# Batch norm with ReLU: small first pieces of x, and stores issued from ScalarE's queue

## The chip, the cores and the metric

One core of one Trainium2 chip. The metric is device microseconds of a whole execution, the median over repeated runs. All timed runs here are in the fast state with a granted clock of 1.0, and the kernel before runs beside every experiment on the same chip. A profile gives the *span*, from the first to the last instruction, which is 1.7 to 2.1 us shorter than the time, depending on the kernel. Ratios are the mean time of one kernel's fast runs over that of the other's of the same rounds, so not quite the ratio of the medians that are quoted.

## The reference

```python
x: (32, 128, 32, 32) float32; gamma, beta, running_mean, running_var: (128,)
normalized = (x - running_mean[None, :, None, None]) / np.sqrt(running_var[None, :, None, None] + eps)
scaled = normalized * gamma[None, :, None, None] + beta[None, :, None, None]
return np.maximum(scaled, 0)
```

16.8 MB come in and 16.8 MB go out; per element there is one multiply-add and a maximum.

## The kernel before

Each of the 128 partitions takes 16 consecutive rows of 1024 numbers, twice. All of x fits into SBUF, so all loads are issued first. The parameters are spread over the partitions by a small matmul, turned into one scale and one bias per row, and each row is one ReLU ACTIVATE on ScalarE. Loads and stores share SyncE's queue.

```python
J = 16
PIECES = ((0, 8), (8, 16))
...
for t in range(T):                                   # T = 2
    for a, b in PIECES:
        xt = data.tile([P, b - a, HW], F32, name=f"x{t}_{a}")
        nc.sync.dma_start(out=xt, in_=xr[t, :, a:b, :])
        tiles.append((t, a, b, xt))
...                                                  # raw: 4 loads of 0.5 KB on nc.scalar
nc.tensor.matmul(cols..., rep..., raw...)            # then Sqrt, reciprocal, scale_t, bias_t
for t, a, b, xt in tiles:
    for j in range(a, b):
        nc.scalar.activation(out=xt[:, j - a, :], in_=xt[:, j - a, :], func=ACTF.Relu,
                             bias=bias_t[:, j : j + 1], scale=scale_t[:, j : j + 1])
    nc.sync.dma_start(out=outr[t, :, a:b, :], in_=xt)
```

## Time and profile before

| | before |
|---|---|
| time, median of 3 | 84.79 us (84.72 to 84.86) |
| span | 83.2 us |
| 16 DMA engines busy with x and out | 95.5% |
| ScalarE busy | 46% |
| first ReLU, last ReLU ends | 14.9, 52.6 us |
| last load landed, last store landed | 43.4, 82.1 us |

The prediction shows the profile lines behind this and reads them. A data packet here is one partition's share of one DMA: 8 rows of 4 KB make a packet of 32 KB.

### The profile page before, as it was taken

What the parts mean: (1) busy time and instruction counts of PE and PEld (TensorE: products, weight loads), DVE (VectorE), ACT (ScalarE), POOL (GpSimd) and SP (SyncE); (2) the same over time, 40 slices, a digit from 0 to 9 for tenths busy, and PEclk for the clock granted to TensorE, in tenths of its full rate; (3) what the DMA queues carried; (4) which work ended last, traced back from release to release, by engine and by line L of the source; (5) the groups of instructions that cost most, each with busy time, mean ns of one, the idle gap of its engine ahead of it and who ended that gap; (6) DMA issues with size and microseconds to landing.
All of it is one profiled execution on the core that took longest, in us unless ns stands there. A gap on an engine that the chain in (4) does not pass through costs nothing.

```text
span 83.2 us, 115 instructions
## 1 busy us (share of the span) xinstructions
PE 0.7 (1%) x2; PEld 0.5 (1%) x2; DVE 0.8 (1%) x5; ACT 38.0 (46%) x34; POOL 0.8 (1%) x6
## 2 busy tenths in 40 slices
PE   0000003000000000000000000000000000000000
PEld 0000002000000000000000000000000000000000
DVE  0000002100000000000000000000000000000000
ACT  0600001899999999999949999200000000000000
POOL 3000000000000000000000000000000000000000
DMA  5879996997999799899969997998999799899960
GB/s 158 347 331 426 505 457 299 504 504 331 426 504 457 315 489 504 347 410 504 252 284 473 489 457 331 489 489 363 426 489 457 315 489 489 378 410 489 489 268 0
DMA packets 1216, 33.56 MB, mean 404 GB/s; under 512 B 192, under 2 KB 192, under 8 KB 192
## 3 DMA queue, kind: packets, MB, share of 16 engines
q1 hardware_dynamic: 1152, 33.55, 95.5%
q10 hardware_dynamic: 64, 0.00, 0.0%
HBM read 16.78 MB, written 16.78 MB: 404 GB/s over the span
## 4 chain that ended last, share of the span: by engine, by line
DMA 50%; ACT 10%; SPq 1%; ACTq 1%; issue 0%
DMA x<-in_x_dram 50%; ACT x L92 10%; SPq L50 1%; ACTq L130 1%
## 5 line engine op out<-in xcount | busy, mean ns | idle before, releaser
L92 ACT ACTIVATE x<-x,bias_t,scale_t 128x1024 f32<-128x1024 f32 x32 | 36.4, 1226 | 2.2 <-DMA x<-in_x_dram 1.2
L80 ACT ACTIVATE std_t<-cols,eps_t 128x16 f32<-128x16 f32 x1 | 0.3, 273 | 9.8 <-PE cols L72 9.8
L80 ACT ACT_TABLE_LOAD x1 | 1.3, 1283 | 2.6 <-issue 2.6
L72 PE MATMUL cols<-raw,rep 8*128 8x64 f32 x2 | 0.7, 428 | 12.9 <-DMA raw<-in_beta_dram 12.9
L72 PEld LDWEIGHTS cols<-raw,rep 8*128 8x128 f32 x2 | 0.5, 304 | 12.9 <-issue 12.9
L62 POOL TENSOR_SCALAR_AFFINE_SELECT rep<-rep 8x128 f32<-8x128 f32 x1 | 0.4, 393 | 0.1
L82 DVE RECIPROCAL rstd_t<-std_t 128x16 f32<-128x16 f32 x1 | 0.3, 253 | 13.0 <-ACT std_t L80 13.0
L61 POOL MEMSET rep<- 8x128 f32 x1 | 0.2, 194 | 0.3 <-POOLq L116 0.3
L84 DVE TENSOR_TENSOR scale_t<-cols,rstd_t 128x16 f32<-128x16 f32 x1 | 0.2, 174 | 0.1
L86 DVE TENSOR_TENSOR ms_t<-cols,scale_t 128x16 f32<-128x16 f32 x1 | 0.2, 174 | 0.0
L88 DVE TENSOR_TENSOR bias_t<-cols,ms_t 128x16 f32<-128x16 f32 x1 | 0.2, 174 | 0.0
L116 POOL MEMSET const-bfloat16-1.0<- 128x1 bf16 x1 | 0.1, 106 | 0.0
L116 POOL MEMSET const-uint8-127<- 128x1 uint8 x1 | 0.1, 106 | 0.0
L116 POOL MEMSET const-float32-0.0<- 128x1 f32 x1 | 0.1, 103 | 0.3 <-issue 0.3
L116 POOL MEMSET const-float32-1.0<- 128x1 f32 x1 | 0.1, 103 | 0.0
L59 DVE MEMSET eps_t<- 128x1 f32 x1 | 0.1, 59 | 0.9 <-PEq L116 0.9
## 6 DMA issues: line engine op xcount, KB each, us to landing
x<-in_x_dram SPq DMA_DIRECT2D x4, 4096.0 KB, 26.0
out_dram<-x SPq DMA_DIRECT2D x4, 4096.0 KB, 29.6
raw<-in_running_var_dram ACTq DMA_DIRECT2D x1, 0.5 KB
raw<-in_gamma_dram ACTq DMA_DIRECT2D x1, 0.5 KB
raw<-in_running_mean_dram ACTq DMA_DIRECT2D x1, 0.5 KB
raw<-in_beta_dram ACTq DMA_DIRECT2D x1, 0.5 KB
```

Of the source, the lines that this page charges most:

```text
L50: nc.sync.dma_start(out=xt, in_=xr[t, :, a:b, :])
L61: nc.gpsimd.memset(rep, 1.0)
L62: nc.gpsimd.affine_select(out=rep, in_=rep, compare_op=mybir.AluOpType.is_equal, fill=0.0, base=0, pattern=[[0, P // Q], [-1, Q]], channel ...
L72: nc.tensor.matmul(cols.rearrange("p k j -> p (k j)"), rep.rearrange("q r s -> q (r s)"), raw.rearrange("q k j -> q (k j)"), start=True, s ...
L80: nc.scalar.activation(out=std_t, in_=cols[:, 0, :], func=ACTF.Sqrt, bias=eps_t[:, 0:1], scale=1.0)
L82: nc.vector.reciprocal(out=rstd_t, in_=std_t)
L84: nc.vector.tensor_mul(out=scale_t, in0=cols[:, 1, :], in1=rstd_t)
L86: nc.vector.tensor_mul(out=ms_t, in0=cols[:, 2, :], in1=scale_t)
L88: nc.vector.tensor_sub(out=bias_t, in0=cols[:, 3, :], in1=ms_t)
L92: nc.scalar.activation(out=xt[:, j - a, :], in_=xt[:, j - a, :], func=ACTF.Relu, bias=bias_t[:, j : j + 1], scale=scale_t[:, j : j + 1],)
L116: nc = _bacc.Bacc("TRN2", target_bir_lowering=False, num_devices=1)
L130: with _tile.TileContext(nc) as tc:
```

## The change

Its intent: let the first rows arrive early, compute them early and write them while the rest of x is still being loaded.

```diff
-PIECES = ((0, 8), (8, 16))
+PIECES = (((0, 2), (2, 4), (4, 8), (8, 16)), ((0, 8), (8, 16)))
@@
-        for a, b in PIECES:
+        for a, b in PIECES[t]:
@@
-        nc.sync.dma_start(out=outr[t, :, a:b, :], in_=xt)
+        nc.scalar.dma_start(out=outr[t, :, a:b, :], in_=xt)
```

## The prediction

> **What bounds the kernel now.** I read the page from the top: busy shares first, then the queues, then the waits, then stretches of the span.
>
> ```profile
> PE 0.7 (1%) x2; PEld 0.5 (1%) x2; DVE 0.8 (1%) x5; ACT 38.0 (46%) x34; POOL 0.8 (1%) x6
> ...
> q1 hardware_dynamic: 1152, 33.55, 95.5%
> q10 hardware_dynamic: 64, 0.00, 0.0%
> ```
>
> No compute engine is near full; ScalarE, which does all the arithmetic, is busy 46% of 83.2 us. The queue of x and of the results (q1, fed by SyncE) holds the 16 DMA engines for 95.5% of the span. 33.55 MB in 1152 packets is 1024 data packets of 32 KB (8 DMAs of 128 partitions) and 128 closing ones, so 64 data packets per engine.
>
> The waits of SyncE's queue tell the order in which that traffic runs:
>
> ```profile
> SPq L99 <- ACT x L92: 37.4, 4, 11.0
> SPq L130 <- DMA out_dram<-x: 29.2, 1, 29.2
> SPq L99 <- DMA x<-in_x_dram: 11.1, 2, 10.3
> ```
>
> The middle row is the end of the kernel: after the last store is issued, SyncE waits 29.2 us for it to land. ScalarE has long finished; the timeline has its last stretch:
>
> ```profile
> 14.90 27.25 ACT L92 ACTIVATE x<-x,bias_t,scale_t 128x1024 f32<-128x1024 f32 x24 [1.02 <-DVE bias_t L88]
> 24.09 28.81 SPq L99 DMA_DIRECT2D out_dram<-x  x4
> 43.39 9.16 ACT L92 ACTIVATE x<-x,bias_t,scale_t 128x1024 f32<-128x1024 f32 x8 [1.23 <-DMA x<-in_x_dram]
> ```
>
> The first store is issued at 24.09 but stands behind the loads in the same queue, so nothing is written until the last load has landed at 43.4. Compute ends at 43.39 + 9.16 = 52.6, about 30 us before the end. The chain of waits (50% on the loads of x, 10% on ScalarE) stops at that compute and gives no reason for the 30 us after it; the stretches do:
>
> ```profile
> 0.00:1.80 1.80, 0.00 (x0) 0.00 (x0) 0.06 (x1) 0.00 (x0) 0.80 (x6) 1.00 0.00 0
> 1.80:3.60 1.80, 0.00 (x0) 0.00 (x0) 0.00 (x0) 1.05 (x1) 0.00 (x0) 1.00 1.00 291
> 3.60:13.30 9.70, 0.38 (x2) 0.41 (x2) 0.00 (x0) 0.24 (x1) 0.00 (x0) 1.00 1.00 433
> 13.30:23.00 9.70, 0.27 (x2) 0.08 (x1) 0.78 (x4) 8.37 (x9) 0.00 (x0) 1.00 1.00 432
> ...
> 37.50:43.70 6.20, 0.00 (x0) 0.00 (x0) 0.00 (x0) 4.97 (x6) 0.00 (x0) 1.00 1.03 370
> 43.70:53.40 9.70, 0.00 (x0) 0.00 (x0) 0.00 (x0) 8.84 (x8) 0.00 (x0) 1.00 1.00 432
> ```
>
> The last two columns are the DMA share and GB/s. Loads alone run at 432 GB/s, stores alone too, with the engines full. The holes are 1.8 us before the first byte, a slow first packet (1.8 us at 291, so 0.6 us lost), and the handover from loads to stores (6.2 us at 370: 6.2 x (1 - 370/432) = 0.9 us lost). Thus 33.55 MB / 432 GB/s = 77.7 us, plus 1.8, 0.6 and 0.9, is 81.0; the rest, some 2.2 us, is the spread between engines, the last landing and the closing barrier. The kernel is bound by DMA bytes at an already flat rate.
>
> **What the Trainium skill says.** Four places.
> "DMA: Bandwidth & Descriptors", section "Issuing engines are not separate DMA queues": DMAs started from scalar, sync or gpsimd run on the same 16 engines and interleave; a second issuer saves only issue time. The trace agrees as far as it goes: while q10 is served, the stretch 3.60 to 13.30 is at a total of 433 GB/s.
> The same page, "Queues, rings and completion order": each DMA engine goes round-robin over the queues with work, a packet at a time. The trace fits: the parameters are 64 packets on q10, and though the last is issued at 2.08 and is half a KB, the matmul waits for it until 12.9, about one 1.2 us turn per packet.
> The same page, section "Bandwidth", puts the fabric ceiling at 435 GB/s; the 432 above stands at it.
> "Perfetto Trace Analysis", "Per-instruction lifecycle": an ACTIVATE waits for its semaphore in a wait queue while the sequencer reads on, whereas a DMA instruction waits in the sequencer itself. No row of this trace shows what that does to a store queued behind an ACTIVATE.
>
> **The change, part by part.**
> (1) Smaller first loads. The first two are 8 KB per partition, then 16 KB, then 32 KB thrice: 6 loads and 6 stores for 4 and 4. Four more DMAs add closing packets only, far under 0.2 us. A 32 KB packet takes 32768 x 16 / 432e9 = 1.21 us, so an 8 KB one 0.3 us: the parameters, interleaved with those, should arrive between 5 and 9 us instead of 12.9. From matmul start to first ReLU was 14.90 - 12.92 = 2.0 us, so ScalarE starts the ReLUs at 7 to 11 instead of 14.9. That is 4 to 8 us gained on an engine that finishes 30 us early: worth nothing directly.
> (2) Stores on ScalarE's queue. SyncE's loads no longer stand in front. ReLUs start 27.25 / 24 = 1.13 us apart, so the first store (two rows) goes out at 10 to 14 and its bytes run beside the loads. The instruction order shows most stores one ACTIVATE after their piece, with that ACTIVATE waiting for the next load; so a store may go out only when the next piece has landed. An issue takes 0.3 to 0.6 us of ScalarE's sequencer, 6 of them about 2.5 us, off the bounding path.
> (3) Loads get later. Each byte of store taken early pushes a load back. With alternating packets, an 8 KB store packet gets a fifth of the bytes beside 32 KB loads. Stepping the packets by hand in this order, the last load lands near 50 us instead of 43.4. By then (50 - 2) x 432 = 20.7 MB have moved, 16.8 of loads, 3.9 of stores; 12.9 MB of stores, 30 us of work, are left, against 9.2 us of ReLUs and some 3 us of landing and issue for the last piece. DMA does not run dry.
> (4) Two late loads now wait for parameter semaphores that they reuse. Those arrive by 9 us, and the loads issued before them last until about 22 us: no hole.
> Sum: bytes unchanged, 77.7 us; start and end unchanged; the handover of 0.9 us is either paid again when mixing begins, or saved: 0 to -0.9; packets and issues +0.1. Median 84.0 to 84.9.
>
> **The rivals.**
> A: mixing costs rate. The handover shows loads slowed while stores begin to be fetched. If it is paid again for each 32 KB of store that runs beside loads, about 8 packets per engine before 50 us (3.9 MB / 16 / 32 KB), it is 8 x 0.9 = 7 us: about 92. A fraction of it is as plausible, 86 to 88. For: those 0.9 us appear only where the directions meet. Against: a one-time filling of the engine's buffer would look the same. The before trace has no steady mix, so this is the real uncertainty.
> B: bytes rather than packets are shared evenly. Then half the rate goes to stores from 12 us, the last load lands at about 68, nearly all other stores are written by then, and the last piece's 9.2 us of ReLUs stand bare ahead of its 9.7 us store: span about 91. The parameters' one-by-one delay speaks against it.
> C: stores fall behind in ScalarE's queue because of the ACTIVATE ahead. The backlog of 30 us hides it; it would cost only if B held too.
> D: overlap gains. All it could win is handover 0.9 and a slow first packet 0.6, together 1.5 us, or 1.8%: under the 2% line.
>
> **Range and chances.** The centre is 84.7: no net change, a little of the handover saved, a little mixing loss. Low 83.2 is D in full; high 88.5 leaves room for half of A. Faster by over 2% needs under 83.1, beyond D: 0.05. A or B in full or by a third gives slower: 0.28. The rest, 0.67, is the same.
>
> **What the changed profile would show.** Right: parameters landing well before 12.9, ReLUs from 7 to 11 us, ScalarE busy still 38 us but spread to near 60 with waits for loads, reads and writes mixed from about 12 us at 425 to 432 GB/s, last load near 50, DMA share at 95%, the end again a wait for a store to land. A shows as a lower rate with the DMA share still full, in the mixed stretch alone. B shows as a late last load (past 60) and a hole in DMA ahead of the last store. The prediction is wrong if the mixed stretch holds under 415 GB/s, or if any hole over 1.5 us opens.

## The result, and the profile after

The changed kernel takes 84.17 us (84.12 to 84.31, 4 runs) against 84.83 (84.72 to 84.89, 4 runs) before: ratio 0.9927, 95% interval 0.991 to 0.9944. It is a small gain of 0.7%, clear of noise and inside the 2% band. The span fell from 83.2 to 82.3 us.

Everything that the change was meant to do, it did. First the two queues of the changed kernel, which now share the traffic:

```profile
q1 hardware_dynamic: 864, 16.78, 48.6%
q10 hardware_dynamic: 928, 16.78, 47.5%
```

48.6% and 47.5% together are 96.1%: the engines were full before and are full now. Then its waits by engine (us in total, times, longest); the first row is ScalarE waiting for loads, the second the matmul waiting for the parameters:

```profile
ACT x L92 <- DMA x<-in_x_dram: 14.4, 3, 6.3
...
PE cols L72 <- DMA raw<-in_beta_dram: 7.4, 1, 7.4
```

The parameters came at 7.4 us instead of 12.9. ScalarE now waits 14.4 us for loads, where it waited 1.2: it computes the first pieces early and is then held up by loads that share the engines with stores. The timeline shows the same (start, length, instruction, in square brackets the idle time before it):

```profile
9.38 3.50 ACT L92 ACTIVATE x<-x,bias_t,scale_t 128x1024 f32<-128x1024 f32 x3 [1.03 <-DVE bias_t L88]
11.78 0.38 ACTq L99 DMA_DIRECT2D out_dram<-x  x1
...
24.87 9.16 ACT L92 ACTIVATE x<-x,bias_t,scale_t 128x1024 f32<-128x1024 f32 x8 [6.33 <-DMA x<-in_x_dram]
37.00 1.24 ACT L92 ACTIVATE x<-x,bias_t,scale_t 128x1024 f32<-128x1024 f32 x1 [2.97 <-DMA x<-in_x_dram]
37.00 0.34 ACTq L99 DMA_DIRECT2D out_dram<-x  x1
...
51.21 1.24 ACT L92 ACTIVATE x<-x,bias_t,scale_t 128x1024 f32<-128x1024 f32 x1 [5.05 <-DMA x<-in_x_dram]
51.21 0.34 ACTq L99 DMA_DIRECT2D out_dram<-x  x1
...
60.39 0.34 ACTq L99 DMA_DIRECT2D out_dram<-x  x1
```

ReLUs start at 9.38 and the first store goes out at 11.78, against 14.90 and 24.09. But the last load lands at 51.2 instead of 43.4, and the last store is issued at 60.39, where it was 52.6 before. Early work at one end has become late work at the other, as it must when the engines have no spare time. Note also the pairs at 37.00 and 51.21, to which experiment 3 returns: the fourth piece was computed by 24.87 + 9.16 = 34.03, yet its store went out at 37.00, with the ACTIVATE ahead of it.

The stretches tell whether mixing costs rate (last column GB/s):

```profile
13.30:52.10 38.80, 0.00 (x0) 0.00 (x0) 0.00 (x0) 24.45 (x22) 0.00 (x0) 1.00 1.02 432
52.10:71.50 19.40, 0.00 (x0) 0.00 (x0) 0.00 (x0) 8.26 (x8) 0.00 (x0) 1.00 1.00 432
```

432 GB/s with loads and stores mixed, 432 with stores alone.

**Where 0.9 us of span went.** One part is at the very end. SyncE closes the kernel by checking the DMA semaphores, mostly two at a time. Here is that row of the kernel before, then of the changed one (columns: shortest, median and longest in ns, then first and last start in us):

```profile
L130 SPq EVENT_SEMAPHORE  x7: 17/28/28, 82.1 to 83.1; - x7
```

```profile
L130 SPq EVENT_SEMAPHORE  x7: 17/28/28, 52.4 to 82.2; - x7
```

Before, the last store's semaphore was in the first pair, so all checks stood after its landing: 82.07 to 82.41 in the trace, 0.34 us. After, the earlier stores' semaphores are checked as they land, and 0.08 us follow the last landing. That is 0.26 us, a by-product of how many DMAs share eight semaphores. The remaining 0.63 us is the last landing, 82.07 before and 81.44 after.

To see what moved the landing, I summed the trace's packet records. In the steady state a packet takes 1.213 us (32 KB), 0.611 (16 KB), 0.309 (8 KB) or 0.159 (4 KB), whichever way it goes; the 64 KB packets, in biglast alone, take 2.418. *Handover loss* is what data packets that start after 6 us took over these times, divided by 16 engines; nearly all of it lies where stores begin or where their packets change size. It is the loads that pay: in the changed kernel all of the 0.56 is in load packets, while every store packet keeps its steady time, and in the other runs with two queues stores have 0.01 of it at most (biglast 0.08). *Small packets* is what those steady times add to the time of the same bytes at 32 KB (8 KB: 0.309 against 1.213 / 4 = 0.303).

| profiled run, us | before | after |
|---|---|---|
| handover loss per engine | 1.09 | 0.56 |
| excess in the first 6 us | 0.59 | 0.44 |
| small packets | 0 | 0.26 |
| last store landed, mean of the 16 engines | 81.62 | 81.09 |
| last store landed, slowest engine | 82.07 | 81.44 |
| checks after it | 0.34 | 0.08 |

So the mean landing came 0.53 earlier: 0.53 from the handover and 0.15 from the start, less 0.26 for small packets, and 0.11 that I could not place. The 0.15 is not sure: biglast starts with the same loads and has 0.52 in its first 6 us, not 0.44. The slowest engine came 0.11 closer to the mean. The last rows add up to the span's 0.89. The time of the two profiled runs fell by less, 84.87 to 84.21, or 0.66: time less span is 1.71 before and 1.94 after. This belongs to the kernel and repeats in its runs: it is near 1.9 to 2.0 in after, graded_stores and biglast, near 2.0 to 2.1 in reversed, graded_16k and graded_fine, and near 1.7 in the other eight. Those six send their stores from ScalarE's queue, but so do queue_only and one_row, at 1.7; the cause stays open. Times of kernels from different groups thus differ by 0.2 to 0.35 us for a reason outside the span, so where that matters the spans are compared too.

### The profile page after: what moved, and what is told of

The parts are those of the page before. It is cut to its first block, busy times and chain, and to the rows that moved or that the text cites. A ratio compares the mean times of both kernels' runs of the same rounds, so it can differ in the third digit from the quotient of the medians.

```text
span 82.3 us, 117 instructions
## 1 busy us (share of the span) xinstructions
PE 0.7 (1%) x2; PEld 0.5 (1%) x2; DVE 0.8 (1%) x5; ACT 38.2 (46%) x34; POOL 0.8 (1%) x6
## 3 DMA queue, kind: packets, MB, share of 16 engines
q1 hardware_dynamic: 864, 16.78, 48.6%
q10 hardware_dynamic: 928, 16.78, 47.5%
## 4 chain that ended last, share of the span: by engine, by line
DMA 60%; ACT 10%; ACTq 1%; issue 1%
DMA x<-in_x_dram 53%; ACT x L92 10%; DMA raw<-in_beta_dram 6%; ACTq L57 1%
## 5 line engine op out<-in xcount | busy, mean ns | idle before, releaser
L92 ACT ACTIVATE x<-x,bias_t,scale_t 128x1024 f32<-128x1024 f32 x32 | 36.6, 1227 | 15.4 <-DMA x<-in_x_dram 14.4
```

## The experiments

Theory H, stated first: the gain is a cheaper handover from reading to writing, because stores begin beside the loads, plus the closing checks. Rival E: the gain comes from parameters and ReLUs that are 5.5 us earlier. After the first four runs came theory F on the size of the handover loss: it is store data fetched ahead while loads still write, so it is small where the first store packets are small. All twelve kernels gave correct results.

| kernel | time, us | ratio to before (95%) | handover loss | small packets | last landing | checks |
|---|---|---|---|---|---|---|
| after | 84.17 | 0.9927 (0.991 to 0.9944) | 0.56 | 0.26 | 81.44 | 0.08 |
| 1 pieces_only | 84.57 | 0.997 (0.9958 to 0.9982) | 1.16 | 0.26 | 82.00 | 0.08 |
| 2 queue_only | 85.13 | 1.0046 (1.0023 to 1.0069) | 1.15 | 0 | 82.17 | 0.34 |
| 3 swapped | 84.04 | 0.9904 (0.9891 to 0.9918) | 0.68 | 0.26 | 81.59 | 0.08 |
| 4 reversed | 84.70 | 0.9985 (0.9971 to 0.9998) | 0.88 | 0.26 | 81.76 | 0.08 |
| 5 graded_stores | 84.28 | 0.994 (0.9925 to 0.9954) | 0.65 | 0.13 | 81.35 | 0.20 |
| 6 one_row | 84.52 | 0.9955 (0.9934 to 0.9976) | 0.16 | 0.40 | 81.98 | 0.25 |
| 7 two_handovers | 85.15 | 1.0033 (1.002 to 1.0046) | 1.66 | 0 | 82.47 | 0.34 |
| 8 biglast | 88.87 | 1.0479 (1.0463 to 1.0495) | 0.74 | 0.13 | 85.90 | 0.20 |
| 9 closing_order | 87.05 | 1.0264 (1.025 to 1.0279) | 1.79 | 0 | 84.41 | 0.08 |
| 10 graded_16k | 84.44 | 0.9956 (0.9942 to 0.997) | 0.60 | 0.07 | 81.31 | 0.27 |
| 11 graded_fine | 84.55 | 0.9966 (0.9952 to 0.9979) | 0.99 | 0.27 | 81.80 | 0.08 |
| 12 fine_swapped | 84.31 | 0.9937 (0.9924 to 0.995) | 0.85 | 0.27 | 81.77 | 0.08 |

The last four columns are of one profiled run each, so a tenth in them should not be leaned on. The loss of closing_order includes a restart after a hole.

**1. pieces_only: the small pieces, stores back on SyncE's queue.**

```diff
-        nc.scalar.dma_start(out=outr[t, :, a:b, :], in_=xt)
+        nc.sync.dma_start(out=outr[t, :, a:b, :], in_=xt)
```

> The small first loads, but all stores on SyncE's queue behind the loads. Theory H (the gain is a cheaper handover between reading and writing, because stores begin beside the loads, plus about 0.3 us of the closing waits): no mixing, so the handover of 0.9 us is paid as before and the time is 84.5 to 84.9. Rival E (the gain comes from the parameters and the ReLUs being 5.5 us earlier): the whole gain stays, 84.1 to 84.3. Both expect the first ReLU near 9.4 us and the last load landed near 43.

Measured 84.57, in H's range. ReLUs start early here too, at 9.47 us, so E is out: early compute by itself gives nothing. Loads and stores do not mix, the handover costs 1.16, and the last store lands at 82.00, as before. What is left, 0.3% or 0.26 us, is just what the closing checks lost: 0.08 us of them instead of 0.34.

**2. queue_only: the old pieces, stores on ScalarE's queue.**

```diff
-PIECES = (((0, 2), (2, 4), (4, 8), (8, 16)), ((0, 8), (8, 16)))
+PIECES = ((0, 8), (8, 16))
```

> The old four 32 KB-per-partition pieces, stores on ScalarE's queue. ReLUs start at 14.9 again, the first store goes out near 24. Theory H: reads and writes mix from 25 us, one 32 KB packet each in turn, last load near 55 us, time 84.1 to 84.4, with one loss at the start of mixing. Rival E: no gain, 84.7 to 84.9. Rival A of the prediction (a loss at every change between reading and writing): about 8 us more, some 92. A hole in DMA before the last store is expected by neither H nor E.

Measured 85.13: a miss for H, whose overlap was there but brought nothing. The stretches show why:

```profile
25.00:31.20 6.20, 0.00 (x0) 0.00 (x0) 0.00 (x0) 6.20 (x6) 0.00 (x0) 1.00 0.97 338
31.20:55.40 24.20, 0.00 (x0) 0.00 (x0) 0.00 (x0) 11.56 (x11) 0.00 (x0) 1.00 1.00 433
55.40:79.60 24.20, 0.00 (x0) 0.00 (x0) 0.00 (x0) 9.16 (x8) 0.00 (x0) 1.00 1.00 433
```

The handover loss has only moved, from 40 us to the moment when mixing begins; in packets it is 1.15 against 1.09. After it, load and store packets of 32 KB run side by side for 24 us, 16 of each in every 2.4 us or one of each per engine, at 433 GB/s. That is the clean answer to rival A of the prediction: in the steady state mixing costs nothing. So neither half of the change gives the gain by overlap alone: pieces without the queue save only checks, the queue without pieces saves nothing. The profiled run is the fastest of the six (84.97, the slowest took 85.60), so what makes the others slower than the kernel before is not in this trace.

**3. swapped: loads from ScalarE, parameters and stores from SyncE.**

```diff
-            nc.sync.dma_start(out=xt, in_=xr[t, :, a:b, :])
+            nc.scalar.dma_start(out=xt, in_=xr[t, :, a:b, :])
@@
-        nc.scalar.dma_start(out=raw[:, k, :], ...)
+        nc.sync.dma_start(out=raw[:, k, :], ...)
@@
-        nc.scalar.dma_start(out=outr[t, :, a:b, :], in_=xt)
+        nc.sync.dma_start(out=outr[t, :, a:b, :], in_=xt)
```

> The changed kernel with queues exchanged: loads issued by ScalarE, parameters and stores by SyncE. In the changed kernel two stores were held until the next ACTIVATE got its load (3.0 and 5.1 us after their piece was computed); here nothing stands ahead of a store, so each should go out within 0.2 us of its piece's last ReLU. Theory H with the hold off the path: same time, 84.1 to 84.4. Rival C (the hold costs): 1 to 5 us faster, 79 to 83.

The stores of the fourth and fifth piece went out at 34.01 and 46.14 us, as soon as they were computed, where the changed kernel held them to 37.00 and 51.21. The timeline of this run:

```profile
34.01 12.47 SPq L99 DMA_DIRECT2D out_dram<-x  x2
36.96 9.16 ACT L92 ACTIVATE x<-x,bias_t,scale_t 128x1024 f32<-128x1024 f32 x8 [2.98 <-DMA x<-in_x_dram]
```

The time is 84.04, within 0.2% of the changed kernel, with intervals that overlap; the spans are 82.2 to 82.4 here and 82.2 to 82.3 there. So the hold is real, and it is off the path: other stores were waiting in the queue in the meantime.

**4. reversed: pieces of 8, 4, 2, 2.**

```diff
-PIECES = (((0, 2), (2, 4), (4, 8), (8, 16)), ((0, 8), (8, 16)))
+PIECES = (((0, 8), (8, 12), (12, 14), (14, 16)), ((0, 8), (8, 16)))
```

> The changed kernel with the first half of x in pieces of 8, 4, 2, 2 rows, not 2, 2, 4, 8: the same packets and queues in another order. The parameters should arrive at 12.8 and the ReLUs start near 14.9 as before the change, the first store near 24. Theory H: mixing still begins beside the loads, 84.1 to 84.4. Rival E (early ReLUs are the gain): 84.7 to 84.9.

Measured 84.70, a miss for H and the number that E named; but experiment 1 had early ReLUs and no gain from them. Part of the miss lies outside the span: the spans of the six runs (82.5 to 82.8) are on average 0.45 below those of the kernel before, the time only 0.13. The first store packets are 32 KB here, as in queue_only, and the loss is 0.88. This is what led to theory F: what counts may be the size of the packets with which stores begin beside the loads.

**5. graded_stores: the old loads; only the first piece's store is split.** Parameters at 12.9 and ReLUs at 14.9 us, as before the change.

```diff
+        chunks = ((0, 2), (2, 4), (4, 8)) if (t, a) == (0, 0) else ((0, 8),)
+        for c, d in chunks:
+            for j in range(a + c, a + d): ...          # the ReLUs of these rows
-        nc.sync.dma_start(out=outr[t, :, a:b, :], in_=xt)
+            nc.scalar.dma_start(out=outr[t, :, a + c : a + d, :], in_=xt[:, c:d, :])
```

> The kernel before with its four 32 KB loads, stores on ScalarE's queue, and only the store of the first piece split in 2, 2 and 4 rows. Packet times so far, summed over what 8, 16 and 32 KB packets take in the steady state: handover loss 1.1 us per engine in the kernel before, 1.1 with pieces only, 1.15 with the queue only, 0.9 reversed, 0.5 in the changed kernel. Theory F (the loss is store data fetched ahead while loads still write, so it is small where the first store packets are small and alternate with loads): loss about 0.5, last store landed near 81.2, time 84.0 to 84.4, though ReLUs start at 14.9 and the parameters land at 12.8. Rival S (small first loads or early ReLUs are needed too): loss about 1.1, time 84.6 to 85.1.

84.28: nearly the whole gain, with none of the early start. The loss is 0.65, against 1.15 in queue_only, from which this kernel differs in the split of one store. Small first loads, early parameters and early ReLUs are not needed. Its timeline has the late start and the small first store:

```profile
14.86 3.50 ACT L94 ACTIVATE x<-x,bias_t,scale_t 128x1024 f32<-128x1024 f32 x3 [1.02 <-DVE bias_t L88]
17.25 0.37 ACTq L101 DMA_DIRECT2D out_dram<-x  x1
```

**6 and 10. Smaller and larger first store packets.** one_row starts with 4 KB, graded_16k with 16 KB. The edit of one_row, to the changed kernel:

```diff
-PIECES = (((0, 2), (2, 4), (4, 8), (8, 16)), ((0, 8), (8, 16)))
+PIECES = (((0, 1), (1, 2), (2, 4), (4, 8), (8, 16)), ((0, 8), (8, 16)))
```

> The changed kernel with its first piece split in two of one row: first store packets of 4 KB, not 8. Theory F: the first loss, 0.36 us in the changed kernel, goes to about 0.2, and 8 more pairs of small packets cost about 0.05: time within 0.2 us of the changed kernel, 84.0 to 84.2. Rival G (the loss has a floor, whatever the size): no gain and a little overhead, 84.2 to 84.4.

The edit of graded_16k, to graded_stores:

```diff
-        chunks = ((0, 2), (2, 4), (4, 8)) if (t, a) == (0, 0) else ((0, 8),)
+        chunks = ((0, 4), (4, 8)) if (t, a) == (0, 0) else ((0, 8),)
```

> Graded stores with the first piece's store in 4 and 4 rows, so first store packets of 16 KB. Theory F (loss grows with the first store packets: 0.16 us at 4 KB, 0.56 to 0.74 at 8 KB, 0.9 to 1.15 at 32 KB): loss 0.7 to 0.9, time 84.3 to 84.7. If only packets of 8 KB and less help: loss 1.1, 84.7 to 85.0.

In one_row the handover loss is 0.16, the lowest of all, and yet the median is 84.52, with runs from 84.07 to 84.69: a miss in time for F and for G. The gain was paid back elsewhere. Small packets cost 0.40; and the first loads of 4 KB start slowly. These are the first 3 us of its loads, then of the changed kernel's:

```profile
1.80:4.85 3.05, 0.00 (x0) 0.00 (x0) 0.00 (x0) 1.28 (x1) 0.00 (x0) 1.00 0.83 259
```

```profile
1.80:4.85 3.05, 0.00 (x0) 0.00 (x0) 0.00 (x0) 1.28 (x1) 0.00 (x0) 1.00 0.95 344
```

The DMA share is 0.83 against 0.95, so in that stretch the engines stood partly idle. In the profiled run the slowest engine also landed 0.66 after the mean, against 0.34; but that run is the slowest of the six, so the others need not have this. graded_16k came out at 84.44, in F's range, with a loss of 0.60, a little under what F gave for it. First packets of 16 KB do as well as those of 8 KB, which F did not expect: the spans are 82.3 to 82.4 here and 82.3 to 82.5 in graded_stores, and the 0.16 between the times lies outside them.

**7. two_handovers: one queue, load, load, load, store, load, store, store, store.**

```diff
+            if (t, a) != (1, 8):
                 nc.sync.dma_start(out=xt, in_=xr[t, :, a:b, :])
@@
         nc.sync.dma_start(out=outr[t, :, a:b, :], in_=xt)
+        if (t, a) == (0, 0):
+            last = tiles[3][3]
+            nc.sync.dma_start(out=last, in_=xr[1, :, 8:16, :])
```

> The kernel before, all on SyncE's queue, with the first store put ahead of the last load: load, load, load, store, load, store, store, store. No mixing, but loads change to stores twice. Theory F and my reading of the handover: each change from loads to stores costs about 1.1 us per engine, and the one from stores to loads nothing or up to the 0.6 of the first packets: last store landed 83.2 to 83.8, time 85.9 to 86.5. If the loss were one of filling up once for the whole kernel, 84.7 to 84.9.

85.15, a miss for the expected 85.9 to 86.5, and above the 84.7 to 84.9 of a loss paid once. Of the 1.66 lost, 1.43 lie at the first change to stores (25 to 35 us) and only 0.20 at the second (50 to 55). The stretches have the first at 346 GB/s and the second at the full rate:

```profile
26.70:34.00 7.30, 0.00 (x0) 0.00 (x0) 0.00 (x0) 6.72 (x7) 0.00 (x0) 1.00 1.00 346
50.90:53.30 2.40, 0.00 (x0) 0.00 (x0) 0.00 (x0) 0.00 (x0) 0.00 (x0) 1.00 1.10 437
```

In this run the loss is not a fee for each change of direction: most of it is paid once. That fits something that is filled up once and stays filled, but no run here shows what is filled.

**8. biglast: the second half of x as one piece of 16 rows.** It takes away the cover of the last ReLUs.

```diff
-PIECES = (((0, 2), (2, 4), (4, 8), (8, 16)), ((0, 8), (8, 16)))
+PIECES = (((0, 2), (2, 4), (4, 8), (8, 16)), ((0, 16),))
```

> The changed kernel with the second half of x as one piece of 16 rows. The last ReLUs then take 16 x 1.13 = 18.1 us after a landing near 47, while the stores left by then (the first half, less what was mixed in) last only until about 61 to 62. The backlog argument of the prediction: DMA runs dry for 4 to 5 us before the last store, time 88 to 89.5. If the compute were hidden whatever its size: 84 to 84.5.

Measured 88.87, inside the expected 88 to 89.5. The timeline has the last ReLUs and the last store, the stretches the hole:

```profile
46.93 18.20 ACT L92 ACTIVATE x<-x,bias_t,scale_t 128x1024 f32<-128x1024 f32 x16 [13.04 <-DMA x<-in_x_dram]
65.16 0.34 ACTq L99 DMA_DIRECT2D out_dram<-x  x1
```

```profile
60.00:65.50 5.50, 0.00 (x0) 0.00 (x0) 0.00 (x0) 5.13 (x5) 0.00 (x0) 1.00 0.19 83
```

The stores that were ready ran out, and the DMA share is 0.19 until the last store starts. This is the bound under which the changed kernel stays: its last ReLUs end 9.2 us after the last landing, while the stores that were ready by then last until 71.8.

**9. closing_order: the kernel before, with four spare loads of 0.5 KB to shift the semaphores.**

```diff
+    spare = params.tile([Q, 4, J], F32, name="spare")
+    for k in range(4):
+        nc.scalar.dma_start(out=spare[:, k, :], in_=gamma.rearrange("(q j) -> q j", j=J))
```

> The kernel before with four spare loads of 0.5 KB, so that the semaphores fall out as in the changed kernel. In the kernel before, SyncE closes by checking the semaphores two at a time and meets the last store's first: 0.34 us of checks follow the last landing; where the last store's comes last it was 0.08. Expected: last store landed near 82.1 as before, checks 0.08 after it, time 84.5 to 84.65. If the closing checks are not the cause of the 0.25 us that pieces only gained: 84.75 to 84.9.

The checks fell to 0.08 as foreseen, but the time is 87.05, a failed design. With 16 DMAs on eight semaphores, the second load of x was given the first load's and had to wait for it, as the waits of SyncE's queue show:

```profile
SPq L50 <- DMA x<-in_x_dram: 11.8, 1, 11.8
```

It was issued at 13.03, when the first load had landed and nothing else was queued:

```profile
12.10:14.60 2.50, 0.65 (x2) 0.50 (x2) 0.53 (x3) 0.27 (x1) 0.00 (x0) 1.00 0.70 197
```

That hole hides the 0.26 us. So the gain from the checks rests on pieces_only, where the last landing is unchanged and the time falls by 0.3%.

**11 and 12. graded_fine and fine_swapped: an attempt to beat all others.** The edit is to graded_stores.

```diff
-        chunks = ((0, 2), (2, 4), (4, 8)) if (t, a) == (0, 0) else ((0, 8),)
+        chunks = {(0, 0): ((0, 1), (1, 2), (2, 4), (4, 8)),
+                  (0, 8): ((0, 4), (4, 8))}.get((t, a), ((0, 8),))
```

fine_swapped also exchanges the queues, as in experiment 3.

> An attempt to beat both: four 32 KB loads, stores of 1, 1, 2, 4, 4, 4, 8, 8 rows on ScalarE's queue. Theory F: handover loss 0.2 to 0.3 (first packets 4 KB, each step a doubling), small packets 0.25 where the changed kernel has 0.26, closing checks 0.08: mean landing near 80.9, time 83.8 to 84.1. If the loss is only moved to the later steps of size: 84.2 to 84.5.

> The same with queues exchanged: loads from ScalarE, parameters and stores from SyncE, so no store is held behind an ACTIVATE. Theory F: as graded_fine, 83.8 to 84.1, stores issued within 0.2 us of their last ReLU. A gain of over 0.3 us on graded_fine would say that the hold costs after all.

Both miss: 84.55 and 84.31. Mixing began at a loss of only 0.14 and 0.10 (15 to 20 us), but 0.80 and 0.74 were lost between 40 and 45 us, where the loads ended while the stores went over to 8 KB packets. The loss was moved, as the second half of the expectation for graded_fine had it. fine_swapped is 0.24 us faster than graded_fine, clear of noise, but its expectation had set over 0.3 as the sign of a hold that costs, and the spans do not differ (82.5 to 82.6, 82.4 to 82.6): the difference is in time less span, 1.71 against 2.04. Theory F in its simple form, that the first packets alone decide, has fallen. What stands: kernels whose stores began beside the loads with 8 or 16 KB packets lost 0.56 to 0.74, those that began with 32 KB or did not mix, and went over to stores once and without a hole, lost 0.88 to 1.16, and with 4 KB it was 0.16 once and 0.85 to 0.99 twice. What decides it stays open. Nothing here beat the changed kernel by more than 0.2%: swapped, at 84.04, is the lowest.

## Why the prediction was right

- **Bound.** "The kernel is bound by DMA bytes at an already flat rate": the changed kernel moves its mixed stretch at 432 GB/s, the rate from which the prediction started. biglast and closing_order, which open holes in it, lose 4 and 2.3 us.
- **Part 1.** Parameters were put at 5 to 9 us and came at 7.4, ReLUs at 7 to 11 and came at 9.38. That this was "worth nothing directly" is shown by pieces_only.
- **Part 2 and rival C.** The first store was due at 10 to 14 and went out at 11.78. The prediction left open what becomes of a store behind a waiting ACTIVATE. Two of the six were held, by 3.0 and 5.1 us, and swapped shows that this is free.
- **Part 3.** Last load near 50: 51.2. Backlog enough: there was no hole, and biglast shows the hole when it is not.
- **Part 4.** SyncE waited 3.1 and 0.9 us for parameter semaphores that loads reuse, had issued its last load by 7.6 us, and left no hole.
- **Rivals A and B.** A would have taken up to 7 us; queue_only, at 433 GB/s for 24 us of mixed packets, refutes it. B's sign was a last load past 60 us and a hole ahead of the last store; the load landed at 51.2 and there is no hole.
- **The sum.** "0 to -0.9" for the handover measured -0.53 (of 1.09 by packets, where the prediction's 0.9 is from GB/s). Two terms were mis-sized. "packets and issues +0.1" was 0.26, all of it packets: an 8 KB packet takes 0.309, not 0.303. And "start and end unchanged" missed the closing checks, -0.26, a start shorter by 0.15 in the profiled run, and the 0.23 that came on outside the span. That these four make +0.08 together, where +0.1 was forecast, is luck. The median of 84.17 falls inside "84.0 to 84.9"; the centre of 84.7 was 0.5 too high, since it saw "a little" of the handover saved and "a little mixing loss", and half of the handover was saved while the steady mix cost nothing. Two slips in the arithmetic change nothing: 84.79 less 1.5 is 83.3, not 83.2, and 3.9 MB / 16 / 32 KB is 7.4 packets, not 8.

## What to carry to other kernels

When the DMA engines are full from the first byte to the last, earlier compute and overlapped stores only move waiting from one end to the other; look for what is left in the holes of the rate, and expect no more than their sum. Check before splitting that stores which are ready outlast the last piece's compute, and that a load is not made to wait on a semaphore that an earlier transfer holds: those two mistakes cost more here (4.0 and 2.3 us against the kernel before) than the whole change gained. A gain under 1% can be an accident of the closing checks, or of what lies outside the span, so account for both before crediting the idea.

## What the Trainium skill lacked or had wrong

- "Perfetto Trace Analysis", "Per-instruction lifecycle": it has the sequencer go on once an ACTIVATE is in the wait queue. In the changed kernel a store whose piece was done at 34.03 us went out at 37.00, 4 ns after an ACTIVATE that had waited for a load, with no separate semaphore instruction between the two; from another engine's queue it went out at 34.01. (The kernel's text has the store first; the instruction order that the prediction read has that ACTIVATE ahead of it.)
- "DMA: Bandwidth & Descriptors": no section has the loss when an engine goes from loads to stores. It was 1.09 us per engine before, mostly paid once (1.43, then 0.20, in two_handovers), while a steady mix of 32 KB load and store packets ran at 433 GB/s.
- The same page, "Why small descriptors are slow (HBM only)", gives a fixed overhead of about 3 cycles per packet; an estimate, if the page's 850 MHz fabric clock is meant, is 3.5 ns. Here 8 KB packets took 0.309 us and 32 KB packets 1.213, so four small ones cost 0.023 us more, or about 8 ns for each additional packet. No run here shows whether a packet of the trace is a packet of the page.
- No page has the order of a kernel's closing semaphore checks: 0.34 us after the last landing when its semaphore is in the first pair (before), 0.08 when it is in the last (after).
